# An encoder layer on one core: a second buffer for the raw weights and their sums, another order of seven products, and final norms written in place

## The chip, the cores and the metric

The kernel runs on one core of a Trainium2 chip. The metric is device time in microseconds (us) of one execution of the whole program. The engines named below are PE (TensorE, matmuls), PEld (its weight loads), DVE (VectorE), ACT (ScalarE), POOL (GpSimd) and SP (SyncE, which here only issues DMAs). Each engine works through its own queue in order; semaphores tie the queues together.

## The reference, cut to what matters

One bidirectional hybrid layer: latent attention beside a state space model, an output projection, then an MLP with a squared ReLU. The change touches only what stands from the output projection on:

```python
    h = h + rms_norm(mix @ w_out[i], g_post_mix[i])
    m = rms_norm(h, g_pre_mlp[i]) @ w_mlp_up[i]
    m = jnp.square(jax.nn.relu(m)) @ w_mlp_down[i]
    h = h + rms_norm(m, g_post_mlp[i])
return h[:, N_META:]
```

`h` has 2048 rows of 1024 columns (after the 16 meta rows are dropped), `w_mlp_up` is 1024 x 4096, `w_mlp_down` 4096 x 1024, all float32.

## The kernel before

**Precision.** Every float32 operand is split (`split`, lines 125 to 127) into a rounded part (ACT copies it, line 126) and the rest (DVE subtracts, line 127); a product is then three matmuls: high x high, high x low, low x high. In the names, `ah`/`al` and `wh`/`wl` are the two parts of a left and a right factor.

**Seven products.** Both MLP projections multiply 2 x 2 blocks with seven products instead of eight. The sums that the scheme needs are formed ahead (POOL, line 1266 for the up-projection's weights into `st`, line 1555 for the down-projection's into `wst`) and behind (DVE, POOL on the results).

**Up-projection.** The 2048 rows are two halves (`ct` 0 and 1). The activations, transposed and written to DRAM as `HTD`, are read back in four slices of 1 MB (`s_load`, tile `traw`, pool `tst` with 3 buffers), split, and summed (`b_slice`, `t_slice`, `t4_slice`) into the 28 resident pairs of tiles `TB`. Over them run 16 pairs of 128 columns of `w_mlp_up` for each half, 32 pairs in all. Most pairs are `up_pair` (line 1380 on): seven products of 12 matmuls, 84 in all, into PSUM banks pA, pB, pA, pB, pE, pF, pE. Pairs 0 and 16 are `up_pair_c` (96 matmuls in eight products, which start while slices are still being made), pair 15 is `up_pair_k` (84, ordered by slice so that slices of the next half can follow).

The factors of a pair are made by `up_prep` (line 1249 on): it loads 1 MB of weights into `raw`, forms the sums in `st` on POOL, and splits seven factors into `ah`/`al`. Pool `wraw` holds `raw` and `st` with **one** buffer each; `apool` holds nine factors. The next load of `raw` can start only when the last factor of the pair before is out of the buffer.

The results go through squared ReLU (`relu2`, lines 1352 to 1374): ACT twice, then two sums on DVE (lines 1367, 1369) and two on POOL (1371, 1373), so that the seven left factors of the down-projection are written to DRAM as `MD`, seven DMAs (line 1359) for each pair, from tiles `r` (8 buffers).

**Down-projection.** `parts` runs over 8 blocks `b` of 512 rows of `w_mlp_down` and, inside, 4 groups `g` of 512 rows of the result: 32 parts of 84 matmuls (`down`, line 1619 on; matmuls at line 1642). Each part works on two pairs of row tiles (`tp`) and makes seven products into banks A, B, A, B, E, F, E. Behind a product the results go into `acc`, which holds the whole output in SBUF: product 0 is copied by ACT (line 1648); 1 and 3 are added to that copy by DVE into `u` (lines 1650, 1659), and for `b > 0` POOL adds `u` into `acc` (line 1652 after product 1, lines 1661 and 1662 after product 3); DVE adds products 2, 4, 5, 6 (lines 1657, 1664, 1666, 1668). Line 1664 needs what line 1661 wrote. `m_factors` reads `MD` back (tile `mraw`) and splits, `w_factors` loads and makes the right factors of block `b + 1` during `g == 3`, two for each product, into a ring of `WR = 16` (14 are in use).

**Final norms.** In the last block `finish` (line 1597 on) runs once for each of the 16 row tiles: it loads the residual `HD`, squares `acc` on ACT into the second half of its buffer `fin` (line 1604), gets the scale on POOL, multiplies (DVE line 1611; ACT 1614 and POOL 1615 for the other half), adds the residual (DVE line 1616) and writes out (line 1617). There are two buffers `fin`, one for each tile in work.

A scheduler orders each engine's instructions when the program is built; the order in the code is only its starting point.

Of the kernel before, what the change touches and what calls it, by code (L numbers as in the profile page):

```python
# [51 lines left out]
def hymba_layer_kernel(  # L52
# [1119 lines left out]
    tst = hw.enter_context(pool("tst", 3))  # L1172
    wraw = hw.enter_context(pool("wraw", 1))
# [109 lines left out]
    for t in range(NT):  # L1283
        last.append((t, out_tile(t, lambda: hn_T(*last.pop(0)) if len(last) == 2 else None)))
        if t in (10, 11, 12):
            s_load(0, t - 10)
        if t >= NT - 4:
            facs.append(next(prep))
# [9 lines left out]
    upr = up_.enter_context(pool("upr", 8, "right"))  # L1298
# [14 lines left out]
    def t_slice(ct, k, eng=V):  # L1313

        raw = RAW.pop((ct, k))
        b11, b12, _, b22 = (raw[:, i] for i in range(4))
        t1, t2, t3 = rt(), rt(), rt()
        eng.tensor_tensor(out=t1, in0=b12, in1=b11, op=ALU.subtract)
        eng.tensor_tensor(out=t3, in0=b22, in1=b12, op=ALU.subtract)
        eng.tensor_tensor(out=t2, in0=b22, in1=t1, op=ALU.subtract)  # L1320
        if k == 0:
            s_load(ct, 3)
        for n, t in ((T2, t2), (T3, t3), (T1, t1)):
            split(t, *TB[n, k])
# [27 lines left out]
    def relu2(c, src, n, odd, half):  # L1352

        S.activation(out=c, in_=src, func=AF.Relu)
        S.activation(out=c, in_=c, func=AF.Square)
        md = MD[n // NP, n % NP]

        def put(i, x):
            Y.dma_start(out=md[:, i], in_=x)

        if (odd, half) != (0, 1):
            put({(0, 0): 0, (1, 0): 2, (1, 1): 5}[odd, half], c)
        blocks[odd, half] = c
        if len(blocks) == 4:
            a11, a12, a21, a22 = (blocks.pop(x) for x in ((0, 0), (1, 0), (0, 1), (1, 1)))
            s1, s2, s4 = rt(), rt(), rt()
            V.tensor_tensor(out=s1, in0=a21, in1=a22, op=ALU.add)
            put(4, s1)
            V.tensor_tensor(out=a21, in0=a11, in1=a21, op=ALU.subtract)
            put(3, a21)  # L1370
            G.tensor_tensor(out=s2, in0=s1, in1=a11, op=ALU.subtract)
            put(1, s2)
            G.tensor_tensor(out=s4, in0=a12, in1=s2, op=ALU.subtract)
            put(6, s4)
# [132 lines left out]
    for k in range(3):  # L1507
        s_load(1, k)
# [18 lines left out]
    WR = 16  # L1527
# [3 lines left out]
    def w_factors(b):  # L1531
# [9 lines left out]
        for first, *more in ((b11,), (b22, (sub, b12), (add, b11)), (b21,), (b22, (sub, b12)), (b12, (sub, b11)),  # L1541
# [55 lines left out]
    def finish(t):  # L1597
        both = wr.tile([128, 2, 1024], F32, tag="raw", name="fin")
        ht, jk = both[:, 0], both[:, 1]
        Y.dma_start(out=ht, in_=HD[t])  # L1600
        ss = sm.tile([128, 2], F32, tag="s2f", name="s2f")
        for half in range(2):
            hs = slice(half * 512, (half + 1) * 512)
            S.activation(out=jk[:, hs], in_=acc[:, t, hs], func=AF.Square, accum_out=ss[:, half:half + 1])
        st = sm.tile([128, 1], F32, tag="ss", name="ss")
        G.tensor_tensor(out=st, in0=ss[:, 0:1], in1=ss[:, 1:2], op=ALU.add)
        r = rstd_of(st, D)
        for half, eng in ((0, V), (1, G)):
            hs = slice(half * 512, (half + 1) * 512)
            if half == 0:  # L1610
                V.scalar_tensor_tensor(out=jk[:, hs], in0=acc[:, t, hs], scalar=r, in1=gpl[:, hs],
                                       op0=ALU.mult, op1=ALU.mult)
            else:
                S.activation(out=jk[:, hs], in_=acc[:, t, hs], func=AF.Copy, scale=r)
                G.tensor_tensor(out=jk[:, hs], in0=jk[:, hs], in1=gpl[:, hs], op=ALU.mult)
            V.tensor_tensor(out=jk[:, hs], in0=jk[:, hs], in1=ht[:, hs], op=ALU.add)  # L1616
            Y.dma_start(out=ov[t // 8, t % 8][:, hs], in_=jk[:, hs])

    def down(b, g, step):
# [6 lines left out]
        names = ("A", "B", "A", "B", "E", "F", "E")  # L1626
        p = [{} for _ in range(2)]
        tmp = [{n: dt_.tile([128, 512], F32, tag=n, name=n) for n in ("p1", "u2", "u3")} for _ in range(2)]
        lo, hi = slice(0, 512), slice(512, 1024)
        for i in range(7):  # L1630
            step(i, False)
            first = i in (0, 1, 4, 5)
            mh, ml = mine[i]
            for tp in range(2):
                if first:
                    p[tp][names[i]] = pa("p" + names[i])
                ps = p[tp][names[i]]
                for fp in range(2):
                    wh, wl = WF[i][fp]
                    c = 2 * fp + tp  # L1640
                    for j, (x, y) in enumerate(((mh, wh), (mh, wl), (ml, wh))):
                        T.matmul(out=ps, lhsT=x[:, c], rhs=y, start=(first and fp == 0 and j == 0),  # L1642
                                 stop=(fp == 1 and j == 2), skip_group_check=not first)
                ta, tb_ = tiles[tp]
                p1, u2, u3 = (tmp[tp][n] for n in ("p1", "u2", "u3"))
                c11, c12, c21, c22 = acc[:, ta, lo], acc[:, ta, hi], acc[:, tb_, lo], acc[:, tb_, hi]
                if i == 0:
                    S.copy(out=p1, in_=ps)
                elif i == 1:
                    V.tensor_tensor(out=u2, in0=ps, in1=p1, op=ALU.add)  # L1650
                    if b > 0:
                        G.tensor_tensor(out=c12, in0=c12, in1=u2, op=ALU.add)
                elif i == 2:
                    if b == 0:
                        S.copy(out=c11, in_=ps)
                    else:
                        V.tensor_tensor(out=c11, in0=ps, in1=c11, op=ALU.add)
                elif i == 3:
                    V.tensor_tensor(out=u3, in0=ps, in1=p1, op=ALU.add)
                    if b > 0:  # L1660
                        G.tensor_tensor(out=c22, in0=c22, in1=u3, op=ALU.add)  # L1661
                        G.tensor_tensor(out=c21, in0=c21, in1=u3, op=ALU.add)  # L1662
                elif i == 4:
                    V.tensor_tensor(out=c22, in0=ps, in1=u3 if b == 0 else c22, op=ALU.add)
                elif i == 5:
                    V.tensor_tensor(out=c21, in0=u3 if b == 0 else c21, in1=ps, op=ALU.subtract)
                else:
                    V.tensor_tensor(out=c12, in0=ps, in1=u2 if b == 0 else c12, op=ALU.add)
# [59 lines left out]
```

## Time and profile before

| | us |
|---|---|
| three executions, median | 3359.68 (3353.49 to 3363.93) |
| profiled execution, device time | 3362.8 |
| its span, first to last instruction | 3361.0 |

The span of the profiled execution leaves 1.8 us around it. The stages, by the lines that run: up to about 1855 us attention, state space model and output projection; from there to about 2636 us the up-projection; from there to the end the down-projection, whose last 105 us also hold the final norms. A view "by windows" gives, for each stretch, the length, the busy time and number of instructions of each engine, the granted TensorE clock, the DMA share and GB/s. A matmul's busy time overlaps its neighbours', so the distance from one start to the next is what it costs.

### The profile page before, as it was taken

What the parts mean: (1) busy time and instruction counts of PE and PEld (TensorE: products, weight loads), DVE (VectorE), ACT (ScalarE), POOL (GpSimd) and SP (SyncE); (2) the same over time, 40 slices, a digit from 0 to 9 for tenths busy, and PEclk for the clock granted to TensorE, in tenths of its full rate; (3) what the DMA queues carried; (4) which work ended last, traced back from release to release, by engine and by line L of the source; (5) the groups of instructions that cost most, each with busy time, mean ns of one, the idle gap of its engine ahead of it and who ended that gap; (6) DMA issues with size and microseconds to landing.
All of it is one profiled execution on the core that took longest, in us unless ns stands there. A gap on an engine that the chain in (4) does not pass through costs nothing. (4 is left out here: it accounts for less than half of the span.)

```text
span 3361.0 us, 43408 instructions
## 1 busy us (share of the span) xinstructions
PE 3039.4 (90%) x14095; PEld 2376.0 (71%) x14095; DVE 2258.6 (67%) x3259; ACT 1763.1 (52%) x3329; POOL 1813.4 (54%) x2707
## 2 busy tenths in 40 slices
PE   6999988989999999999798789888899899999995
PEld 5899855656777666787576567666677677777773
DVE  6333387667888766754465755566555678889888
ACT  4333357888777899754354443443434433333343
POOL 4122337776888876100122655557556446767776
PEclk8999989999999999999899899989999899999997
DMA  4222221210000132222465433333333433333345
GB/s 149 66 75 82 78 51 41 52 44 24 26 26 15 47 91 74 87 82 63 117 182 171 138 126 119 131 117 140 132 126 122 143 116 112 118 111 115 114 124 179
DMA packets 300452, 329.93 MB, mean 98 GB/s; under 512 B 38736, under 2 KB 240848, under 8 KB 299200
## 3 DMA queue, kind: packets, MB, share of 16 engines
q1 hardware_dynamic: 298176, 325.44, 31.9%
q8 instruction: 111, 1.82, 0.2%
q10 hardware_dynamic: 1792, 1.57, 0.2%
q14 instruction: 117, 0.96, 0.1%
q0 software_dynamic: 256, 0.14, 0.0%
HBM read 206.47 MB, written 120.52 MB: 97 GB/s over the span
## 5 line engine op out<-in xcount | busy, mean ns | idle before, releaser
L628 DVE TENSOR_TENSOR pl<-s,ph 128x512 fp32r<-128x512 f32 x512 | 350.1, 686 | 164.6 <-ACT s L627 159.3
L624 ACT ACTIVATE ph<-s 128x512 fp32r<-128x512 f32 (+1 forms) x544 | 323.4, 595 | 174.5 <-PE s L622 161.1
L575 DVE TENSOR_REDUCE mx<-mxp 128x1 f32<-128x512 f32 x512 | 342.8, 684 | 62.0 <-PE mxp L574 59.0
L1266 POOL TENSOR_TENSOR st<-raw 128x512 f32<-128x512 f32 x120 | 182.7, 1523 | 259.6 <-DMA raw<-in_w_mlp_up_dram 166.7
L627 ACT ACTIVATE s<-s 128x512 f32<-128x512 f32 x512 | 304.0, 594 | 0.7
L126 ACT CAST ah<-mraw 128x512 fp32r<-128x512 f32 x224 | 138.5, 621 | 289.9 <-DMA mraw<-MD 241.1
L127 DVE TENSOR_TENSOR al<-mraw,ah 128x512 fp32r<-128x512 f32 x224 | 235.3, 1052 | 54.9 <-ACT ah L126 50.6
L620 PE MATMUL s<-ql,kh 96*128 96x512 f32 (+1 forms) x544 | 226.3, 416 | 13.2 <-ACT ZS L938 4.9
L612 PE MATMUL X<-pl,vt 128*65 128x512 f32 x512 | 209.6, 409 | 30.2 <-DVE pl L628 28.4
L621 PE MATMUL s<-qh,kl 96*128 96x512 f32 (+1 forms) x544 | 218.0, 401 | 0.0
L622 PE MATMUL s<-qh,kh 97*128 97x512 f32 (+1 forms) x544 | 214.9, 401 | 0.7 <-DMA qh<-nm 0.7
L127 DVE TENSOR_TENSOR al<-st,ah 128x512 fp32r<-128x512 f32 x120 | 127.6, 1064 | 127.7 <-ACT ah L126 123.9
L574 PE MATMUL mxp<-kh,qh 96*128 96x512 f32 x512 | 200.3, 413 | 12.8 <-DVE mx L575 5.1
L132 POOL TENSOR_SCALAR rs_v<-ss 128x1 f32<-128x1 f32 (+1 forms) x98 | 20.5, 209 | 350.8 <-ACT kvn L325 119.0
L613 PE MATMUL X<-ph,vt 128*64 128x512 f32 x512 | 205.4, 401 | 0.0
L614 PE MATMUL X<-ph,vt 128*65 128x512 f32 x512 | 204.6, 400 | 0.0
L126 ACT CAST ah<-st 128x512 fp32r<-128x512 f32 x120 | 74.4, 620 | 208.4 <-POOL st L1266 208.2
L1555 POOL TENSOR_TENSOR wst<-raw 128x512 f32<-128x512 f32 x64 | 97.5, 1529 | 103.0 <-DVE wl L127 91.8
L127 DVE TENSOR_TENSOR al<-raw,ah 128x512 fp32r<-128x512 f32 x98 | 105.9, 1083 | 65.7 <-ACT ah L126 65.7
L620 PEld LDWEIGHTS s<-ql,kh 96*128 96x128 f32 (+1 forms) x544 | 103.5, 190 | 60.2 <-ACT ZS L938 7.1
L574 PEld LDWEIGHTS mxp<-kh,qh 96*128 96x128 f32 x512 | 100.2, 197 | 51.3 <-DVE mx L575 8.1
L648 POOL DMA_DIRECT2D rr<-RD x4 | 2.7, 663 | 246.2 <-DMA RD<-o 135.7
(970 smaller groups left out, 9950.8 us busy)
## 6 DMA issues: line engine op xcount, KB each, us to landing
MD<-r SPq DMA_DIRECT2D x224, 256.0 KB
mraw<-MD SPq DMA_DIRECT2D x224, 256.0 KB
raw<-in_w_mlp_up_dram SPq DMA_DIRECT2D x32, 1024.0 KB
xt<-in_x_dram SPq DMA_DIRECT2D x32, 512.0 KB
raw<-in_w_mlp_down_dram SPq DMA_DIRECT2D x16, 1024.0 KB
ug<-UD SPq DMA_DIRECT2D x32, 256.0 KB
HD<-o SPq DMA_DIRECT2D x16, 512.0 KB
traw<-HTD SPq DMA_DIRECT2D x8, 1024.0 KB
```

What stands on the lines that cost most here:

```text
L126: S.copy(out=h, in_=src)
L127: eng.tensor_tensor(out=l, in0=src, in1=f(h), op=ALU.subtract)
L574: T.matmul(out=p, lhsT=qs[n][0][0:96, j * 128:(j + 1) * 128], rhs=kh[0:96, b * 512:(b + 1) * 512])
L575: V.reduce_max(out=mxs[n][:, j, b:b + 1], in_=p, axis=AX.X)
L612: T.matmul(out=X[:65], lhsT=v[:, t, 0:65], rhs=pl_, start=(t == 0), stop=False)
L613: T.matmul(out=X[:64], lhsT=v[:, t, 65:129], rhs=ph_, start=False, stop=False)
L620: T.matmul(out=s[:m], lhsT=kh[0:96, cs], rhs=ql, start=True, stop=False)
L621: T.matmul(out=s[:m], lhsT=kl[:, cs], rhs=qh[0:96], start=False, stop=False)
L622: T.matmul(out=s[:m], lhsT=kh[:, cs], rhs=qh, start=False, stop=True)
L624: S.activation(out=ph_[:m], in_=s[:m], func=AF.Exp, scale=SCALE)
L627: S.activation(out=s, in_=s, func=AF.Exp, scale=SCALE)
L628: V.tensor_tensor(out=pl_, in0=s, in1=f(ph_), op=ALU.subtract)
```

## The change

1. Pool `wraw` gets two buffers (so two `raw` and two `st`), `tst` two instead of three, `upr` (tiles `r`) seven instead of eight. Slices 2 and 3 of a half are loaded when slices 0 and 1 have been used up. For the first half slice 1's sums move ahead of slice 2's splits.
2. The seven left factors in `MD` and the seven right factors get another order, and `down` uses banks X, Y, X, E, X, F, E. Bank X is read three times: after products 0, 2 and 4. Product 0 goes straight into `acc` (DVE adds for `b > 0`, ACT copies for `b == 0`), so do 1, 2 and 3; only product 4 is copied by ACT into a tile `x3`, which POOL adds twice. POOL's adds for each pair of tiles fall from three to two for `b > 0`; DVE's stay at six.
3. The ring of right factors grows to 18, and four of the 14 for the next block are made in group 2.
4. `finish` takes two row tiles for one buffer, keeps only the residual and the result there, squares into `x3` and multiplies in `acc`. In the last part the products of the first pair of tiles run before those of the second.

```diff
-    tst = hw.enter_context(pool("tst", 3))
-    wraw = hw.enter_context(pool("wraw", 1))
+    tst = hw.enter_context(pool("tst", 2))
+    wraw = hw.enter_context(pool("wraw", 2))
...
-        if t in (10, 11, 12):
+        if t in (10, 11):
             s_load(0, t - 10)
...
-    upr = up_.enter_context(pool("upr", 8, "right"))
+    upr = up_.enter_context(pool("upr", 7, "right"))
...
-        if k == 0:
-            s_load(ct, 3)
+        if k < 2:
+            s_load(ct, k + 2)
...
     t_slice(0, 0, G)
-    b_slice(0, 2)
+    t_slice(0, 1, G)
 
     def before(k):
         if k == 1:
             hn_T(*last.pop(0))
-            t_slice(0, 1, G)
+            b_slice(0, 2)
...
-    for k in range(3):
+    for k in range(2):
         s_load(1, k)
...
-    WR = 16
+    WR = 18
...
-        for first, *more in ((b11,), (b22, (sub, b12), (add, b11)), (b21,), (b22, (sub, b12)), (b12, (sub, b11)),
+        for first, *more in ((b11,), (b21,), (b22, (sub, b12), (add, b11)), (b12, (sub, b11)), (b22, (sub, b12)),
                              (b22, (sub, b12), (add, b11), (sub, b21)), (b22,)):
...
-    def finish(t):
+    def finish(ts_):
+
         both = wr.tile([128, 2, 1024], F32, tag="raw", name="fin")
-        ht, jk = both[:, 0], both[:, 1]
-        Y.dma_start(out=ht, in_=HD[t])
...
+        for i, t in enumerate(ts_):
+            Y.dma_start(out=both[:, i], in_=HD[t])
+        for i, t in enumerate(ts_):
+            ht = both[:, i]
+            ss = sm.tile([128, 2], F32, tag="s2f", name="s2f")
+            for half in range(2):
+                hs = slice(half * 512, (half + 1) * 512)
+                S.activation(out=dt_.tile([128, 512], F32, tag="x3", name="jk"), in_=acc[:, t, hs], func=AF.Square,
+                             accum_out=ss[:, half:half + 1])
...
+                c = acc[:, t, hs]
+                if half == 0:
+                    V.scalar_tensor_tensor(out=c, in0=c, scalar=r, in1=gpl[:, hs], op0=ALU.mult, op1=ALU.mult)
+                else:
+                    S.activation(out=c, in_=c, func=AF.Copy, scale=r)
+                    G.tensor_tensor(out=c, in0=c, in1=gpl[:, hs], op=ALU.mult)
+                V.tensor_tensor(out=ht[:, hs], in0=c, in1=ht[:, hs], op=ALU.add)
+                Y.dma_start(out=ov[t // 8, t % 8][:, hs], in_=ht[:, hs])
...
-        names = ("A", "B", "A", "B", "E", "F", "E")
+        banks = "XYXEXFE"
...
+            def put(c):
+                if b == 0:
+                    S.copy(out=c, in_=ps)
+                else:
+                    V.tensor_tensor(out=c, in0=ps, in1=c, op=ALU.add)
+
+            if i == 0:
+                put(c11)
+            elif i == 1:
+                V.tensor_tensor(out=c11, in0=ps, in1=c11, op=ALU.add)
+            elif i == 2:
+                put(c12)
+            elif i == 3:
+                put(c22)
+            elif i == 4:
+                p[tp]["x"] = x3 = dt_.tile([128, 512], F32, tag="x3", name="x3")
+                S.copy(out=x3, in_=ps)
+                G.tensor_tensor(out=c22, in0=c22, in1=x3, op=ALU.add)
+            elif i == 5:
+                x3 = p[tp]["x"]
+                V.tensor_tensor(out=c21, in0=x3 if b == 0 else c21, in1=ps, op=ALU.subtract)
+                if b > 0:
+                    G.tensor_tensor(out=c21, in0=c21, in1=x3, op=ALU.add)
+            else:
+                V.tensor_tensor(out=c12, in0=ps, in1=c12, op=ALU.add)
+
+        if b == NB - 1 and g == 3:
+            for tp in range(2):
+                for i in range(7):
+                    product(i, tp)
+                finish(tiles[tp])
+            return
...
-        if g == 3:
+        if g == 2:
             nwf = w_factors(b + 1) if b + 1 < NB else iter(())
...
-                if g == 3:
+                if g == 2 and i > 2:
+                    next(nwf, None)
+                elif g == 3:
                     next(nwf, None)
                     next(nwf, None)
```

**SP, first pairs of the up-projection.** A row is an instruction (x6: six alike in a row): `raw` is the weights of a pair, `traw` a slice, `MD<-r` a result. Before, from the last residual row on:

```order
L1275 DMA traw<-HTD 128x2048
L1245 DMA HTD<-raw 128x4x128 x2
L1254 DMA raw<-in_w_mlp_up_dram 128x8x256
L1275 DMA traw<-HTD 128x2048 x3
L1359 DMA MD<-r 128x512 x9
L1254 DMA raw<-in_w_mlp_up_dram 128x8x256
L1359 DMA MD<-r 128x512 x6
L1254 DMA raw<-in_w_mlp_up_dram 128x8x256
L1359 DMA MD<-r 128x512 x7
```

The change, from the same place on:

```order
L1254 DMA raw<-in_w_mlp_up_dram 128x8x256
L1275 DMA traw<-HTD 128x2048
L1245 DMA HTD<-raw 128x4x128 x2
L1254 DMA raw<-in_w_mlp_up_dram 128x8x256
L1275 DMA traw<-HTD 128x2048 x3
L1359 DMA MD<-r 128x512
L1254 DMA raw<-in_w_mlp_up_dram 128x8x256
L1359 DMA MD<-r 128x512 x8
L1254 DMA raw<-in_w_mlp_up_dram 128x8x256 x2
L1359 DMA MD<-r 128x512 x9
L1254 DMA raw<-in_w_mlp_up_dram 128x8x256
L1359 DMA MD<-r 128x512 x7
```

When nine results have been written, one of these loads has been issued before (that of pair 1), and three with the change; after 18 results it is three before, and with the change five, with the sixth next in the queue.

**DVE, one part of the down-projection with `b > 0`.** `al` is the rest of a left factor; `acc` the output; pA, pB, pE, pF, pX, pY the banks. Before:

```order
L1668 TENSOR_TENSOR acc<-pE,acc 128x512 x2
L1650 TENSOR_TENSOR u_29233<-pB,p_29232 128x512
L127 TENSOR_TENSOR al<-mraw,ah 128x512
L1650 TENSOR_TENSOR u_29236<-pB,p_29235 128x512
L127 TENSOR_TENSOR al<-mraw,ah 128x512
L1657 TENSOR_TENSOR acc<-pA,acc 128x512 x2
L127 TENSOR_TENSOR al<-mraw,ah 128x512
L1659 TENSOR_TENSOR u_29234<-pB,p_29232 128x512
L1659 TENSOR_TENSOR u_29237<-pB,p_29235 128x512
L127 TENSOR_TENSOR al<-mraw,ah 128x512
L1664 TENSOR_TENSOR acc<-pE,acc 128x512
```

The change:

```order
L1673 TENSOR_TENSOR acc<-pE,acc 128x512 x2
L127 TENSOR_TENSOR al<-mraw,ah 128x512
L1653 TENSOR_TENSOR acc<-pX,acc 128x512 x2
L127 TENSOR_TENSOR al<-mraw,ah 128x512
L1658 TENSOR_TENSOR acc<-pY,acc 128x512 x2
L127 TENSOR_TENSOR al<-mraw,ah 128x512
L1653 TENSOR_TENSOR acc<-pX,acc 128x512 x2
L1653 TENSOR_TENSOR acc<-pE,acc 128x512
L127 TENSOR_TENSOR al<-mraw,ah 128x512
L1653 TENSOR_TENSOR acc<-pE,acc 128x512
L127 TENSOR_TENSOR al<-mraw,ah 128x512
L1669 TENSOR_TENSOR acc<-acc,pF 128x512 x2
```

Bank X now leaves through DVE after products 0 and 2 (bank A left through ACT after product 0), and no row of DVE up to product 3 reads a sum that POOL made in the same part.

**SP, the end of the program.** `fin<-HD` loads a residual, `out_dram<-fin` writes half a row tile. Before:

```order
L1600 DMA fin<-HD 128x1024
L1617 DMA out_dram<-fin 128x512 x4
L1600 DMA fin<-HD 128x1024 x2
L1617 DMA out_dram<-fin 128x512 x4
L1600 DMA fin<-HD 128x1024 x2
L1617 DMA out_dram<-fin 128x512 x4
```

The change:

```order
L1601 DMA fin<-HD 128x1024 x2
L1621 DMA out_dram<-fin 128x512 x6
L1601 DMA fin<-HD 128x1024 x2
L1621 DMA out_dram<-fin 128x512 x2
L1601 DMA fin<-HD 128x1024 x2
L1621 DMA out_dram<-fin 128x512 x8
```

Before, the last two residuals are loaded behind all but the last four writes; with the change behind all but the last eight.

More of the change, by code (lines that the diff above doesn't have):

```diff
@@ L1361, in relu2 @@
         if (odd, half) != (0, 1):
-            put({(0, 0): 0, (1, 0): 2, (1, 1): 5}[odd, half], c)
+            put({(0, 0): 0, (1, 0): 1, (1, 1): 5}[odd, half], c)
         blocks[odd, half] = c
@@ L1367, in relu2 @@
             V.tensor_tensor(out=s1, in0=a21, in1=a22, op=ALU.add)
-            put(4, s1)
+            put(3, s1)
             V.tensor_tensor(out=a21, in0=a11, in1=a21, op=ALU.subtract)
-            put(3, a21)
+            put(4, a21)
             G.tensor_tensor(out=s2, in0=s1, in1=a11, op=ALU.subtract)
-            put(1, s2)
+            put(2, s2)
             G.tensor_tensor(out=s4, in0=a12, in1=s2, op=ALU.subtract)
@@ L1595, in hymba_layer_kernel @@
     Y.dma_start(out=gpl, in_=g_post_mlp[0].partition_broadcast(128))
-    def finish(t):
+    def finish(ts_):
         both = wr.tile([128, 2, 1024], F32, tag="raw", name="fin")
-        ht, jk = both[:, 0], both[:, 1]
-        Y.dma_start(out=ht, in_=HD[t])
[L1601 to L1617, printed above, removed]
@@ new lines, in finish @@
+        for i, t in enumerate(ts_):
[7 more added lines that the diff above has]
+                             accum_out=ss[:, half:half + 1])
+            st = sm.tile([128, 1], F32, tag="ss", name="ss")
+            G.tensor_tensor(out=st, in0=ss[:, 0:1], in1=ss[:, 1:2], op=ALU.add)
+            r = rstd_of(st, D)
+            for half in range(2):
+                hs = slice(half * 512, (half + 1) * 512)
+                c = acc[:, t, hs]
[6 more added lines that the diff above has]
+                Y.dma_start(out=ov[t // 8, t % 8][:, hs], in_=ht[:, hs])
@@ L1625, in down, with product @@
         del MFs[:7]
-        names = ("A", "B", "A", "B", "E", "F", "E")
+        banks = "XYXEXFE"
         p = [{} for _ in range(2)]
-        tmp = [{n: dt_.tile([128, 512], F32, tag=n, name=n) for n in ("p1", "u2", "u3")} for _ in range(2)]
         lo, hi = slice(0, 512), slice(512, 1024)
+        def product(i, tp):
+            first = i in (0, 1, 3, 5)
+            mh, ml = mine[i]
+            if first:
+                p[tp][banks[i]] = pa("p" + banks[i])
+            ps = p[tp][banks[i]]
+            for fp in range(2):
+                wh, wl = WF[i][fp]
+                c = 2 * fp + tp
+                for j, (x, y) in enumerate(((mh, wh), (mh, wl), (ml, wh))):
+                    T.matmul(out=ps, lhsT=x[:, c], rhs=y, start=(first and fp == 0 and j == 0),
+                             stop=(fp == 1 and j == 2), skip_group_check=not first)
+            ta, tb_ = tiles[tp]
+            c11, c12, c21, c22 = acc[:, ta, lo], acc[:, ta, hi], acc[:, tb_, lo], acc[:, tb_, hi]
+            def put(c):
[22 more added lines that the diff above has]
+                V.tensor_tensor(out=c12, in0=ps, in1=c12, op=ALU.add)
@@ L1630, in down @@
+        if b == NB - 1 and g == 3:
[4 more added lines that the diff above has]
+            return
         for i in range(7):
             step(i, False)
-            first = i in (0, 1, 4, 5)
-            mh, ml = mine[i]
             for tp in range(2):
[L1635 to L1668, printed above, removed]
@@ L1669, in down @@
+                product(i, tp)
             step(i, True)
         if b == NB - 1:
-            for ta, tb_ in tiles:
-                finish(ta)
-                finish(tb_)
+            for pair in tiles:
+                finish(pair)
     parts = [(b, g) for b in range(NB) for g in range(4)]
```

## The prediction

> **What bounds the kernel now.** I read the page's head first, then a view by windows over the two projections, then who makes PE wait there, and last single rows.
>
> ```profile
> span 3361.0 us, 43408 instructions
> PE 3039.4 (90%) x14095; PEld 2376.0 (71%) x14095; DVE 2258.6 (67%) x3259; ACT 1763.1 (52%) x3329; POOL 1813.4 (54%) x2707
> ```
>
> ```profile
> core 0: us, PE busy (x) PEld busy (x) DVE busy (x) ACT busy (x) POOL busy (x), PEclk, DMA share, GB/s
> 1877.00:1915.00 38.00, 24.64 (x87) 17.79 (x85) 31.79 (x30) 16.34 (x30) 29.67 (x20) 0.82 0.42 145
> 1915.00:2215.00 300.00, 269.35 (x1091) 209.22 (x1091) 168.13 (x183) 120.63 (x206) 172.85 (x118) 0.95 0.37 125
> 2215.00:2306.00 91.00, 69.80 (x266) 52.62 (x264) 71.07 (x79) 43.36 (x77) 57.36 (x36) 0.89 0.40 139
> 2306.00:2607.00 301.00, 273.88 (x1092) 213.63 (x1093) 166.77 (x183) 120.23 (x207) 175.51 (x119) 0.94 0.37 124
> 2607.00:2636.00 29.00, 26.17 (x101) 20.12 (x99) 17.62 (x20) 13.87 (x24) 13.09 (x10) 0.88 0.37 122
> 2636.00:2680.00 44.00, 30.52 (x111) 23.10 (x110) 33.12 (x41) 21.52 (x39) 22.61 (x15) 0.84 0.54 172
> 2680.00:2800.00 120.00, 117.34 (x513) 95.51 (x512) 93.31 (x129) 45.95 (x79) 53.13 (x37) 1.00 0.37 112
> 2800.00:3240.00 440.00, 418.99 (x1790) 334.44 (x1789) 388.60 (x477) 153.41 (x264) 314.08 (x205) 0.99 0.38 113
> 3240.00:3361.00 121.00, 73.74 (x282) 55.84 (x280) 100.69 (x114) 47.29 (x107) 83.56 (x88) 0.82 0.52 174
> ```
>
> PE is the busiest engine in all of these stretches, but busy time hides how far the matmuls stand apart. Single rows show that:
>
> ```profile
> 2336.62 0.50 PE L1341 MATMUL pA<-T00h,ah 128*128 128x512 f32 x1 [2.87 <-ACT ah L126]
> 2338.53 0.63 PE L1341 MATMUL pA<-T01h,ah 128*128 128x512 f32 x1
> 2338.95 0.63 PE L1341 MATMUL pA<-T01l,ah 128*128 128x512 f32 x1
> 2344.22 0.39 PE L1341 MATMUL pA<-T20h,ah 128*128 128x512 f32 x1
> 2346.94 0.39 PE L1341 MATMUL pB<-T30h,ah 128*128 128x512 f32 x1
> ```
>
> From 2344.22 to 2346.94 stand the 12 matmuls of one product: 2.72 / 12 = 0.2267 us each. That is the price of a matmul when nothing is missing. Just behind the wait of 2.87 us they stand 0.42 apart, nearly twice as far: a gap is paid again in slow matmuls behind it. By 0.2267, the 513 matmuls of the stretch from 2680 need 116.3 of its 120 us, while the 1092 from 2306 need 247.6 of 301. So the up-projection loses most. Its wait and its rhythm:
>
> ```profile
> PE pA L1341 <- ACT ah L126: 42.5, 22, 3.3
> PE pA L1341 <- DVE al L127: 11.8, 21, 0.6
> ```
>
> ```profile
> 1938.53 0.38 SPq L1254 DMA_DIRECT2D raw<-in_w_mlp_up_dram  x1
> ...
> 2215.25 0.38 SPq L1254 DMA_DIRECT2D raw<-in_w_mlp_up_dram  x1
> ...
> 2306.01 0.38 SPq L1254 DMA_DIRECT2D raw<-in_w_mlp_up_dram  x1
> ...
> 2607.06 0.38 SPq L1254 DMA_DIRECT2D raw<-in_w_mlp_up_dram  x1
> ```
>
> The first fence counts PE's waits from 1915 to 2607: some 22 pairs begin by waiting for their first factor. In the second, loads 3 and 15 lie 276.7 us apart (12 pairs, 23.06 each), loads 18 and 31 301.1 us (13 pairs, 23.16). A pair needs 84 x 0.2267 = 19.04. What ends the wait is the load:
>
> ```profile
> L1266 POOL TENSOR_TENSOR st<-raw 128x512 f32<-128x512 f32 x52 | 76.8, 1477 | 113.6 <-DMA raw<-in_w_mlp_up_dram 74.6 <-DVE al L127 39.0
> L127 DVE TENSOR_TENSOR al<-st,ah 128x512 fp32r<-128x512 f32 x52 | 55.7, 1071 | 64.4 <-ACT ah L126 62.8
> L1266 POOL TENSOR_TENSOR st<-st,raw 128x512 f32<-128x512 f32 x39 | 54.4, 1395 | 3.1
> L127 DVE TENSOR_TENSOR al<-raw,ah 128x512 fp32r<-128x512 f32 x39 | 41.0, 1052 | 29.7 <-ACT ah L126 29.7
> L1367 DVE TENSOR_TENSOR r<-r 128x512 f32<-128x512 f32 x13 | 22.6, 1741 | 0.3 <-ACT r L1355 0.3
> L1371 POOL TENSOR_TENSOR r<-r 128x512 f32<-128x512 f32 x13 | 20.3, 1559 | 8.2 <-DVE r L1367 8.2
> L1373 POOL TENSOR_TENSOR r<-r 128x512 f32<-128x512 f32 x13 | 21.8, 1674 | 0.5
> L1404 DVE TENSOR_TENSOR r<-u,pF 128x512 f32<-128x512 f32 x13 | 8.9, 686 | 6.0 <-PE pF L1341 5.9
> ```
>
> These groups cover the 13 pairs from 2306 to 2607. POOL stands 74.6 / 13 = 5.7 us a pair waiting for `raw`, and 39.0 / 13 = 3.0 for its one buffer `st`. So a pair's cycle is not PE's 19.04: it is one load plus the chain POOL, ACT, DVE over seven factors, with nothing overlapped.
>
> **Term 1, the pairs.** With two `raw`, SP's order shows the loads one to two pairs ahead, so both waits of POOL leave the cycle. Next in line are the engines themselves: POOL has (76.8 + 54.4 + 20.3 + 21.8) / 13 = 13.3 us a pair, DVE 166.8 / 13 = 12.8, ACT 120.2 / 13 = 9.2, all from the rows above. All lie under 19.04, so PE becomes the bound, with nine factor buffers as its reserve. How close it comes I take from the stretch at 2680: 116.3 / 120 = 97%, 19.04 / 0.97 = 19.6. The 601 us of the two windows hold 26 pairs: 26 x (23.1 - 19.6) = **91 us**. At best 26 x 4.06 = 105; the other end is the first rival's, 49.
>
> **Term 2, the change of halves.** The window 2215 to 2306 holds pairs 15, 16 and 17: 264 matmuls, 59.8 us, of 91. Factors made ahead take away some of the 31 us lost, but DVE was busy for 71.1 of them, with splits and sums of the slices that remain. Now slices 2 and 3 also wait for a buffer of 0 and 1, and SP stands behind that, with the writes of `MD` queued after it and only seven `r`. Not shown before: at worst one load in the open, 5.7 us as POOL sees it, at best 25 of the 31. I take **14**, near the middle.
>
> **Term 3, the first pairs.** 87 matmuls, 19.7 us, in the 38 from 1877; DVE is busy for 31.8. Loads 1 and 2 come earlier, slices 2 and 3 later (again at most a load, 5.7); DVE's work is as before. Between -6 and +10 I take **3**.
>
> **Term 4, into the down-projection.** 2607 to 2680: 212 matmuls, 48.1 us, of 73. PE waits there:
>
> ```profile
> PE pB L1642 <- ACT wh L126: 7.3, 1, 7.3
> PE pF L1642 <- ACT wh L126: 5.4, 1, 5.4
> ```
>
> The first is for the second right factor. It was a sum made by POOL and is now a plain block, so that wait should shrink; the second stays a sum that ACT splits between casts. The pair that ends in this stretch also begins with a wait of term 1's kind. **10**, between 0 and 18.
>
> **Term 5, the down-projection.** From 2800 to 3240 1790 matmuls need 405.8 of 440 us. Its waits and the POOL row that goes:
>
> ```profile
> PE pE L1642 <- DVE acc L1664: 8.8, 13, 1.7
> PE pB L1642 <- DVE u L1650: 8.2, 8, 2.0
> ```
>
> ```profile
> L1652 POOL TENSOR_TENSOR acc<-acc,u 128x512 f32<-128x512 f32 x43 | 65.0, 1524 | 56.5 <-DVE u L1650 56.5
> ```
>
> DVE is the second bound here: 388.6 of 440, 88%. It keeps six adds for each pair of tiles, at 0.69 (line 1404's row is such an add). But POOL loses one add of three: 65 us of its 314. And DVE's splits depend on what POOL does beside them:
>
> ```profile
> 2336.05 1.27 POOL L1266 TENSOR_TENSOR st<-raw 128x512 f32<-128x512 f32 x1 [6.34 <-DMA raw<-in_w_mlp_up_dram]
> ...
> 2341.99 1.77 DVE L127 TENSOR_TENSOR al<-raw,ah 128x512 fp32r<-128x512 f32 x1
> ...
> 2347.52 0.69 DVE L127 TENSOR_TENSOR al<-st,ah 128x512 fp32r<-128x512 f32 x1 [1.46 <-ACT ah L126]
> ```
>
> The same split takes DVE 0.69 or 1.77 us; a sum on POOL takes 1.27 when it runs alone and 1477 ns on the mean. With fewer adds on POOL fewer splits are long; the right factors are spread over 11 steps in place of 7, and no bank waits for POOL any more. Of the 34 us lost I take back **20** (5 to 30: the named waits alone are 17).
>
> **Term 6, the end.**
>
> ```profile
> L1604 ACT ACTIVATE fin<-acc 128x512 f32<-128x512 f32 x32 | 19.9, 623 | 44.5 <-DMA out_dram<-fin 39.6 <-DVE acc L1664 2.9 <-DVE acc L1668 1.1
> ```
>
> ACT waits 39.6 us for a buffer whose result is still being written, although it needs it only as scratch. Squaring elsewhere and four tiles in two buffers take that wait away. What is late next is DVE: 100.7 us of work in the 121, all of which stays. So 121 can fall to about 106, with some 5 us of DVE idle in the last chain: **15**, between 3 (another wait takes its place) and 25 (DVE's ops shorter as POOL works less).
>
> **Sum.** 91 + 14 + 3 + 10 + 20 + 15 = 153; all low ends 49 - 6 - 6 + 0 + 5 + 3 = 45, all high ends 213. The profiled execution took 3362.8, 3.1 over the median of 3359.7. So 3362.8 - 153 - 3 = **3207**.
>
> **Rivals.** *DVE and POOL bind the pairs* (3249). Denser pairs put POOL's ops beside more of DVE's. If each of a pair's nine DVE ops on two tiles of SBUF (seven `al`, lines 1367 and 1369) took 1.77, with four adds from a bank at 0.69, DVE would need 18.7 us; at the 88% that it reaches in the down-projection a pair takes 21.2, and term 1 is 26 x 1.9 = 49. The sum is 111. For it: line 1367 stands at 1741 ns already. Against: `al` is at 1.06 on the mean, and seven factors of reserve smooth it. The Trainium skill ("SBUF — State Buffer", section "Who interferes with whom") states a rule that speaks against the change here: DVE and GpSimd share one port pair as an exclusive lock, held for a whole instruction, so that a DVE operation with both inputs in SBUF and a GpSimd operation block each other fully. By that rule a pair whose nine DVE operations all meet a POOL operation is the one of 21.2 us, and the sum is 111; without it the sum is 153. The 1.77 beside the 0.69 agree with it.
>
> *The loads are not ahead after all* (3298). SP issues in order, and a load that waits for its buffer holds back the writes of `MD` behind it; if `r` runs out, the pair stays at 23.1. Only term 1 goes: 3362.8 - 62 - 3. Against: the load has a whole pair of slack, and seven `r` serve seven results a pair.
>
> *Bank X makes PE wait, and the kernel is slower* (3423). Product 2 needs X free of product 0, product 4 of product 2, each with one product (2.72 us) between, and both leave through DVE for `b > 0`, which is 88% busy. If two long splits (2 x 1.77) stand ahead each time, 28 parts x 2 x 3.5 = 196 us come in where term 5 gave 20: 3362.8 - 133 + 196 - 3. It turns the sign from 133 / 56 = 2.4 us a read. Against: bank B had just such a read and waited 8.2 us in 440; for: its longest wait, 2.0, is near the price.
>
> **Chances.** Forecast 0.70, bound by DVE and POOL 0.17, no loads ahead 0.06, bank X 0.04, better than all this 0.03. The range 3150 to 3275 takes in the first two with the uncertain terms of halves, start and end. A measurement tells about 0.3%, 10 us, from no change. Faster 0.93, same 0.03, slower 0.04.
>
> **What would show it.** Term 1: loads of `raw` 19 to 20 us apart, POOL without idle time for `raw`, PE clock near 1.00 from 1915. Term 5: no wait of PE for bank E, short ones for X, `al` under 1.05. Term 6: ACT without waits for `out_dram`, DVE over 90% busy to the end. I am wrong if the loads stay 21 us apart or more, or if PE's waits for X add up to over 20 us.

## The result, and the profile after

| | us | range |
|---|---|---|
| before, 4 runs | 3361.8 | 3353.5 to 3367.8 |
| after, 4 runs | 3232.4 | 3229.2 to 3232.8 |

The ratio is 0.9615, with a 95% interval from 0.9592 to 0.9637: 3.8% faster. The forecast was 3207, in a range from 3150 to 3275, so the time lies in the range, 25 us above the predicted one, which was put together from parts that missed in both directions. One execution of `ring_18_late`, below, ran at a granted clock of 0.743 and took 3671.8 us; its time there is the median of the other four.

The view by windows of the changed kernel, with the columns of before. Its up-projection ends at 2502 instead of 2636, so 2502, 2546, 2666 and 3106 answer to 2636, 2680, 2800 and 3240 of before:

```profile
core 0: us, PE busy (x) PEld busy (x) DVE busy (x) ACT busy (x) POOL busy (x), PEclk, DMA share, GB/s
...
1961.00:2145.00 184.00, 184.00 (x814) 152.38 (x813) 123.83 (x136) 88.47 (x154) 132.55 (x89) 1.00 0.47 152
...
2188.00:2244.00 56.00, 46.43 (x190) 37.00 (x189) 49.56 (x49) 25.86 (x47) 45.20 (x27) 0.91 0.44 147
2244.00:2502.00 258.00, 258.00 (x1140) 213.66 (x1139) 189.08 (x198) 128.62 (x224) 183.44 (x124) 1.00 0.48 156
2502.00:2546.00 44.00, 32.28 (x118) 24.24 (x117) 26.21 (x31) 21.46 (x39) 20.87 (x14) 0.84 0.40 124
2546.00:2666.00 120.00, 114.68 (x489) 93.20 (x489) 90.92 (x113) 48.76 (x86) 52.55 (x36) 0.97 0.39 119
2666.00:3106.00 440.00, 410.86 (x1753) 335.38 (x1752) 365.48 (x473) 151.09 (x263) 239.26 (x157) 0.97 0.37 111
3106.00:3227.00 121.00, 87.27 (x346) 67.34 (x344) 106.59 (x126) 50.33 (x115) 86.46 (x89) 0.89 0.55 185
```

PE has no gap in the pairs: 814 matmuls of 0.2267 us need 184.5 of 184 us, at a granted clock of 1.00. The up-projection, from the last write of `HD` to the down-projection's first matmul, took 782.5 us before (1853.7 to 2636.2) and takes 654.5 (1847.7 to 2502.2), 128 less. From there to the end it was 724.8 us before and is 725.2. So **128 of the 133.6 us between the two profiled executions lie in the up-projection**, and the forecast's 45 us for terms 4 to 6 did not come. The other 6 us lie ahead of it; in the experiments below that start wanders from 1845.7 to 1852.6 (one_raw apart), so they are not put down to the change. Counting matmuls by 0.2267 shows how the last 725 us come out level: the 120 us stretch does 489 instead of 513 (5.4 us worse), the 440 us stretch 1753 instead of 1790 (8.4 worse), the last 121 us 346 instead of 282 (14.5 better). Such counts are good to some 3 us.

Four groups of the page after: the copies (line 126) and splits (line 127) of left factors, the up-projection's sums (line 1266) and the first matmuls into bank X (line 1644). A row has the count, busy us, mean ns, then the idle time before them:

```profile
L126 ACT CAST ah<-mraw 128x512 fp32r<-128x512 f32 x224 | 138.8, 620 | 302.4 <-DMA mraw<-MD 216.0
L127 DVE TENSOR_TENSOR al<-mraw,ah 128x512 fp32r<-128x512 f32 x224 | 214.8, 964 | 73.5 <-ACT ah L126 68.2
L1266 POOL TENSOR_TENSOR st<-raw 128x512 f32<-128x512 f32 x120 | 179.9, 1501 | 135.2 <-DVE al L127 128.5
...
L1644 PE MATMUL pX<-wh,ah 128*128 128x512 f32 x384 | 160.2, 418 | 48.4 <-DVE acc L1653 48.1
```

POOL hardly waits for the load any more (6.7 us of the 135.2, 166.7 before), only for DVE. And PE now waits 48.1 us for bank X, which the forecast named as a sign that it is wrong (over 20 us). Six waits of 2.9 to 5.2 us, one in each block, near its start, make 26 us of it, and the last 121 us another 14. Single rows of one such place, first SP, then ACT, DVE and PE (start, length, engine, line; in brackets the idle time and what ended it):

```profile
2864.89 0.98 SPq L1537 DMA_DIRECT2D raw<-in_w_mlp_down_dram  x2
2866.65 18.32 SPq L1570 DMA_DIRECT2D mraw<-MD  x6
```

```profile
2869.77 1.14 ACT L126 CAST wh<-raw 128x512 fp32r<-128x512 f32 x2 [4.41 <-DMA raw<-in_w_mlp_down_dram]
2872.36 1.14 ACT L126 CAST wh<-raw 128x512 fp32r<-128x512 f32 x2 [1.45 <-DMA raw<-in_w_mlp_down_dram]
...
2881.52 0.62 ACT L126 CAST ah<-mraw 128x512 fp32r<-128x512 f32 x1 [6.01 <-DMA mraw<-MD]
```

```profile
2864.14 1.28 DVE L127 TENSOR_TENSOR wl<-raw,wh 128x512 fp32r<-128x512 f32 x2
...
2870.43 2.99 DVE L127 TENSOR_TENSOR wl<-raw,wh 128x512 fp32r<-128x512 f32 x2 [0.81 <-ACT wh L126]
2873.34 1.27 DVE L1669 TENSOR_TENSOR acc<-acc,pF 128x512 f32<-128x512 f32 x2
2874.54 2.38 DVE L127 TENSOR_TENSOR wl<-raw,wh 128x512 fp32r<-128x512 f32 x2
2876.84 3.48 DVE L127 TENSOR_TENSOR al<-mraw,ah 128x512 fp32r<-128x512 f32 x2
...
2882.17 1.03 DVE L127 TENSOR_TENSOR al<-mraw,ah 128x512 fp32r<-128x512 f32 x1 [0.66 <-ACT ah L126]
2883.88 0.69 DVE L127 TENSOR_TENSOR al<-mraw,ah 128x512 fp32r<-128x512 f32 x1 [0.67 <-ACT ah L126]
2884.49 1.28 DVE L1653 TENSOR_TENSOR acc<-pX,acc 128x512 f32<-128x512 f32 x2
```

```profile
2885.23 0.79 PE L1644 MATMUL pX<-wh,ah 128*128 128x512 f32 x1 [5.17 <-DVE acc L1653]
2885.82 0.63 PE L1644 MATMUL pX<-wl,ah 128*128 128x512 f32 x1
2886.25 0.63 PE L1644 MATMUL pX<-wh,al 128*128 128x512 f32 x1
```

The next block's weights (2 MB) are loaded and at once four right factors are split. DVE's queue holds four `wl` and then splits of left factors. Pairs of these take 2.4 to 3.5 us, where the pair at 2864.14 took 1.28; POOL was idle then, and works beside them from 2869.88 on. The last two splits also wait for ACT (0.66 and 0.67 us), whose copy at 2881.52 had waited 6.01 us for its load. SP could issue that load only at 2878.65, when the first of the two splits at 2876.84 had ended and freed one of the two `mraw` buffers, so a late split makes the next one late. The add that frees X stands behind all this.

### The profile page after: what moved, and what is told of

The parts are those of the page before. It is cut to its first block, busy times and chain, and to the rows that moved or that the text cites. A ratio compares the mean times of both kernels' runs of the same rounds, so it can differ in the third digit from the quotient of the medians.

```text
span 3227.4 us, 43434 instructions
## 1 busy us (share of the span) xinstructions
PE 2976.6 (92%) x14095; PEld 2361.9 (73%) x14095; DVE 2246.5 (70%) x3243; ACT 1763.7 (55%) x3345; POOL 1751.5 (54%) x2659
## 5 line engine op out<-in xcount | busy, mean ns | idle before, releaser
L127 DVE TENSOR_TENSOR al<-mraw,ah 128x512 fp32r<-128x512 f32 x224 | 214.8, 964 | 73.5 <-ACT ah L126 68.2
L1266 POOL TENSOR_TENSOR st<-raw 128x512 f32<-128x512 f32 x120 | 179.9, 1501 | 135.2 <-DVE al L127 128.5
L1666 POOL TENSOR_TENSOR acc<-acc,x 128x512 f32<-128x512 f32 x64 | 101.5, 1588 | 200.2 <-ACT x L1665 200.2
L1644 PE MATMUL pX<-wh,ah 128*128 128x512 f32 x384 | 160.2, 418 | 48.4 <-DVE acc L1653 48.1
L1644 PE MATMUL pX<-wl,ah 128*128 128x512 f32 x384 | 156.7, 408 | 0.5 <-DVE wl L127 0.4
L1644 PE MATMUL pX<-wh,al 128*128 128x512 f32 x384 | 156.2, 407 | 0.0
```

What stands on the lines that cost most here:

```text
L127: eng.tensor_tensor(out=l, in0=src, in1=f(h), op=ALU.subtract)
```

## The experiments

Each kernel was timed beside the kernel before, which had 3358.1, 3359.4 and 3360.2 in the three groups of runs; so the groups agree to about 2 us. The intervals reach some 4 to 5 us to either side, and differences below that are not shown.

| kernel | us | ratio to before, 95% |
|---|---|---|
| up_alone | 3228.2 | 0.9603 to 0.9629 |
| up_and_norms | 3223.3 | 0.9585 to 0.9611 |
| up_and_products | 3220.1 | 0.9567 to 0.9593 |
| ring_16 (up, products, norms) | 3205.8 | 0.9533 to 0.9559 |
| ring_18_late | 3229.4 | 0.9597 to 0.9628 |
| old_norms | 3240.5 | 0.9634 to 0.9660 |
| one_sum | 3242.8 | 0.9642 to 0.9669 |
| one_raw | 3330.8 | 0.9905 to 0.9932 |
| third_add | 3223.5 | 0.9579 to 0.9606 |
| x_by_scalar | 3233.6 | 0.9613 to 0.9639 |
| four_mraw | 3195.1 | 0.9499 to 0.9525 |
| low_halves_gpsimd | 3179.8 | 0.9449 to 0.9478 |

### Which buffer: one_sum and one_raw

```diff
-st = wraw.tile([128, 4, 128], F32, tag="st", name="st")
+st = wraw.tile([128, 4, 128], F32, tag="st", name="st", bufs=1)        # one_sum
-raw = wraw.tile([128, 8, 256], F32, tag="raw", name="raw")
+raw = wraw.tile([128, 8, 256], F32, tag="raw", name="raw", bufs=1)     # one_raw; and so the tile `hn` of the last row tile
```

> The changed kernel, with one buffer for the left factors' sums instead of two (two raw buffers stay). Theory A, the second raw buffer carries the up-projection's gain: the pairs stay at 19.0 to 20.0 us and the time lies between 3232 and 3262 us. Theory B, the second sum buffer carries it, since GpSimd may then go ahead of VectorE's split: the pairs go back to 22 to 23 us and the time to 3320 to 3350 us. If both are needed, the time lies between.

> The changed kernel, with one buffer for the raw left weights instead of two (two sum buffers stay). Theory A, the second raw buffer carries the gain, because the load of a pair's weights no longer starts only behind the last read of the pair before: the pairs go back to 22.5 to 23.1 us, the time to 3232 + 26 x 3.5 = 3323 us or some 18 us more where the change of halves loses its gain too (3341 us). Theory B, the second sum buffer carries it: 19.0 to 20.0 us a pair, 3232 to 3262 us.

POOL's waits from 1961 to 2188 us (total, times, longest), first with one sum buffer, then with one raw buffer:

```profile
POOL st L1266 <- DVE al L127: 41.7, 34, 1.9
...
POOL st L1266 <- DMA raw<-in_w_mlp_up_dram: 6.0, 1, 6.0
```

```profile
POOL st L1266 <- DMA raw<-in_w_mlp_up_dram: 68.1, 11, 6.6
POOL st L1266 <- DVE al L127: 19.7, 16, 1.8
```

With one `raw` the wait is back, 6.2 us a pair (68.1 / 11), and the kernel takes 3330.8, 98 us more than the changed one. Not all of that is the pairs': in the profiled execution the up-projection takes 742.3 us (1868.5 to 2610.9), 88 more, so 88 of the 128 us are lost again. It also starts 21 us later. Its instructions stand in another order from the attention part on, and why that part got longer was not looked into. With one `st` 10 us are lost. Theory A holds; the second sum buffer adds a little.

### The parts apart: up_alone, up_and_norms, up_and_products, old_norms

up_alone is the kernel before with the up-projection's lines of the change, among them these; up_and_norms adds the new `finish` and the last part's loop over `tp`, up_and_products the new order and banks instead. old_norms is the changed kernel without its norms.

```diff
-    tst = hw.enter_context(pool("tst", 3))
-    wraw = hw.enter_context(pool("wraw", 1))
+    tst = hw.enter_context(pool("tst", 2))
+    wraw = hw.enter_context(pool("wraw", 2))
...
-        if k == 0:
-            s_load(ct, 3)
+        if k < 2:
+            s_load(ct, k + 2)
```

> The kernel before with the up-projection's part of the change alone (raw and sum buffers, tiles of the right operand, order of its slices and of the products written out); the down-projection and the final norms are the old ones, and so is the ring of right factors. Theory C, the down-projection's part and the norms together give nothing (the new products lose about 14 us in the middle, the new end gains about 14): 3232 us, within 6. Theory D, by the forecast's terms 4 to 6 the rest is worth 45 us: 3277 us. In the trace theory C wants 790 to 800 matmuls in each 184 us of the steady down-projection or more, as before, and the last 121 us with some 282 matmuls as before instead of 346.

> The kernel before with the up-projection's part of the change and the new final norms (two tiles a buffer, in place, the last part one pair of tiles after the other), but with the old order and old banks of the down-projection's products. Theory C, the new products lose 14 us in the middle and the new end gains 14.5 by itself: 3232 - 14 = 3218 us. Theory E, the end gains only because the new products leave VectorE and GpSimd freer there, so norms and products go together: 3232 us. If the new products gain (forecast's term 5, 20 us): 3252 us.

> The changed kernel with the old final norms (one tile a buffer, beside a second tile) and with the last part's two pairs of tiles side by side in each product, as before the change. By the count of matmuls in the last 121 us the new end is worth 14.5 us: 3247 us, from 3240 to 3255. If the end is set by VectorE's work whatever the order, 3232 us.

> The kernel before with the up-projection's part and the new order of products alone: ring of 16 right factors, made in the last part of a block, and the old final norms with the last part's pairs of tiles side by side. If the products' gain (3223 - 3206 = 17 us at the new norms) stands by itself and the norms are worth 5 to 8 us: 3211 to 3214 us. If products and norms only gain together: 3223 us or more.

up_alone takes 3228.2: what the change does behind the up-projection is worth nothing, or costs 4 us, which is within the noise; theory C holds. (The 790 to 800 matmuls in 184 us that the expectation names are no figure of the kernel before, which has 1790 in 440 us; up_alone has 1798.) The norms alone were worth 4.9 us with the old products (3228.2 to 3223.3), between the two theories, and 8.1 in the changed kernel (old_norms), less than counted in the window. up_and_products, too, lies between its two cases, 8.1 below up_alone. With products and norms, ring_16 takes 3205.8: 22.4 less than up_alone, where 8.1 and 4.9 would give 13.0. That they do more together than apart is likely but not shown: by the ratios it is 23.5 us against 18.1, and each of the four ratios has an interval of 4 to 5 us to either side.

### What the ring costs: ring_16 and ring_18_late

```diff
-    WR = 18
+    WR = 16                                  # ring_16 alone
-        if g == 2:
+        if g == 3:                           # both
             nwf = w_factors(b + 1) if b + 1 < NB else iter(())
...
-                if g == 2 and i > 2:
-                    next(nwf, None)
-                elif g == 3:
+                if g == 3:
```

> The changed kernel with a ring of 16 right factors instead of 18, and the next block's factors made in the last part of a block alone, as before the change. It is the control for the next two runs, for which it frees 8 KB a partition. Theory F, the wider ring did not spread the factors' work (all 14 still stand in two of four parts): within 6 us of 3232, and TensorE's waits for bank X stay at about 70 us. Theory G, the four early factors crowd VectorE where X is read: 3215 to 3226 us and X's waits under 40 us.

> The changed kernel with the ring of 18, but with the next block's factors asked for only in the last part of a block, as before the change. Theory W, the width of the ring alone makes the loss, since the scheduler places a factor as soon as the ring has room: 3226 to 3236 us, as the changed kernel. Theory V, the four early requests make it: 3203 to 3215 us.

The wide ring loses 26.6 us (3232.4 to 3205.8), or 23.6 by ring_18_late; ring_16 is faster than even theory G had it. The requests in the code lose nothing: in ring_18_late's trace DVE, ACT and SP run the same instructions in the same order as in the changed kernel's, so the scheduler places a factor as the ring has room, whenever it is asked for. (The 70 us that some expectations give X's waits is not PE's figure, which is 48.1.) PE's waits for X fall from 48.1 to this in ring_16:

```profile
PE pX L1644 <- DVE acc L1653: 26.2, 17, 4.1
```

The loads of two blocks' weights, four blocks apart, of the changed kernel and of ring_16 give the time of a block:

```profile
2696.97 0.97 SPq L1537 DMA_DIRECT2D raw<-in_w_mlp_down_dram  x2
...
3035.57 0.98 SPq L1537 DMA_DIRECT2D raw<-in_w_mlp_down_dram  x2
```

```profile
2702.40 2.53 SPq L1537 DMA_DIRECT2D raw<-in_w_mlp_down_dram  x2
...
3023.99 0.46 SPq L1537 DMA_DIRECT2D raw<-in_w_mlp_down_dram  x1
```

338.6 / 4 = 84.7 us against 321.6 / 4 = 80.4; a block's 336 matmuls need 76.2. The 4.3 us a block are less than what one big wait for X costs with its slow matmuls (7.3 us, last section). So the wide ring did not spread the factors: it moved two more of a block's 14 up to the very start of the block before, into the rows shown above, where four are split at once; in ring_16 two are. At the place shown, the load that ACT waited for took 2.9 us from issue (2878.65) to copy (2881.52), no longer than the next but one (2883.24 to 2886.12), so the crowd in DVE's queue is the nearer cause there and not the 2 MB of weights. Over the kernel the two were not separated.

### What X waits for: x_by_scalar and four_mraw

Both start from ring_16, which frees their space.

```diff
+                elif i == 3:
+                    V.tensor_tensor(out=c, in0=ps, in1=c, op=ALU.add)
                 else:
-                    V.tensor_tensor(out=c, in0=ps, in1=c, op=ALU.add)
+                    xa = dt_.tile([128, 512], F32, tag="xa", name="xa")
+                    S.copy(out=xa, in_=ps)
+                    V.tensor_tensor(out=c, in0=xa, in1=c, op=ALU.add)
```

```diff
-    mst = ctx.enter_context(pool("mst", 2))
+    mst = ctx.enter_context(pool("mst", 4))
```

> The control, and the first and third product's sums are read out of bank X by ScalarE into a tile (tag xa, two buffers), from which VectorE adds them to acc; only from the second block on, and all sums are still computed. Theory T, TensorE waits since X comes free only after an add that stands behind other work in VectorE's queue: the waits of pX for acc all but vanish (under 10 us of 70) and the time falls by 20 to 50 us against the control. Rival R1, the queues are late because of the two mraw buffers (ScalarE waits for a load, VectorE for ScalarE): ScalarE's copy then stands behind the same wait, and the time stays within 8 us of the control. Rival R2, VectorE's throughput is the bound: no gain, or a loss of up to 20 us, since VectorE keeps its adds.

> The control with four mraw buffers instead of two. Rival R1, the left factors' loads make ScalarE late and by it VectorE: ScalarE's waits for mraw (about 200 us in all) fall under 80 us, the waits of pX for acc under 30 us, and the time falls by 15 to 40 us against the control. Theory T alone (the order in VectorE's queue, whatever the loads): X's waits stay above 50 us, the time within 8 us of the control.

Theory T fell: x_by_scalar is 27.8 us **slower** than ring_16, of the sign that R2 had and beyond its 20 us. PE's waits for X moved to ACT, and the add got dearer, first in x_by_scalar, then in ring_16:

```profile
L1644 PE MATMUL pX<-wh,ah 128*128 128x512 f32 x384 | 154.5, 406 | 24.0 <-ACT xa L1656 22.3 <-DVE acc L1662 1.7
...
L1657 DVE TENSOR_TENSOR acc<-xa,acc 128x512 f32<-128x512 f32 x112 | 113.5, 1014 | 0.0
```

```profile
L1653 DVE TENSOR_TENSOR acc<-pX,acc 128x512 f32<-128x512 f32 x112 | 73.2, 678 | 5.4 <-PE pX L1644 5.4
```

From SBUF the same add takes 1014 ns instead of 678, 40.3 us more in all (113.5 - 73.2). Other groups of DVE got shorter, so that its busy time over the whole kernel rises by 22.0 us (2246.8 to 2268.8 by the pages). Four `mraw` gain 10.8 us, between the numbers of the two theories. Its groups of left factors and of X:

```profile
L126 ACT CAST ah<-mraw 128x512 fp32r<-128x512 f32 x224 | 137.8, 620 | 183.2 <-PE pX L1644 89.0 <-PE pE L1644 39.2 <-PE pY L1644 28.1
...
L1644 PE MATMUL pX<-wh,ah 128*128 128x512 f32 x384 | 153.6, 402 | 18.2 <-DVE acc L1653 18.2
```

ACT's waits for the loads, 196.7 us in ring_16, are no longer among the three largest, so 28 us at most. Yet PE still waits 18.2 us for X, of 26.2: the loads carry a part, and something else the rest.

### Whose time is it: third_add and low_halves_gpsimd

third_add puts one more GpSimd add a pair of tiles into ring_16; low_halves_gpsimd moves three of seven subtractions for right factors from VectorE to GpSimd in four_mraw.

```diff
+                    xd = dt_.tile([128, 512], F32, tag="xd", name="xd")
+                    G.tensor_tensor(out=xd, in0=x3, in1=gpl[:, lo], op=ALU.add)   # third_add
...
-                split(src, h, l)
+                split(src, h, l, V if more else G)                              # low_halves_gpsimd
```

> The run with a ring of 16, and behind each sixth product from the second block on one more GpSimd add of 128 x 512, of x3 and the norm's weights into a tile that nothing reads (56 in all, some 85 us of GpSimd's time): GpSimd has three adds for a pair of tiles again, as before the change. Theory P, the new products gain since GpSimd is freer: 3215 to 3224 us, and TensorE's waits grow. Theory Q, they gain by the order in which banks are read and by fewer waits of VectorE, and GpSimd was never the bound: 3203 to 3210 us.

> The run with four mraw buffers, and the low halves (wl) of the three right factors that are raw blocks are made by GpSimd instead of VectorE (6 of 14 a block, each about 0.7 us of VectorE and about 1.5 us of GpSimd). Theory R2, what is left (about 25 us of TensorE in the steady part) is VectorE's throughput: 3183 to 3192 us. Rival, GpSimd's adds beside VectorE's lengthen VectorE's subtractions and right factors come late: 3195 to 3215 us, with more waits for wl or wst.

third_add takes 17.7 us more than ring_16, as theory P had it. Groups of the page's kind, two of ring_16 and then three of third_add:

```profile
L127 DVE TENSOR_TENSOR al<-mraw,ah 128x512 fp32r<-128x512 f32 x224 | 220.7, 990 | 64.7 <-ACT ah L126 63.9
...
L1653 DVE TENSOR_TENSOR acc<-pX,acc 128x512 f32<-128x512 f32 x112 | 73.2, 678 | 5.4 <-PE pX L1644 5.4
```

```profile
L127 DVE TENSOR_TENSOR al<-mraw,ah 128x512 fp32r<-128x512 f32 x224 | 241.5, 1083 | 57.1 <-ACT ah L126 55.6
...
L1673 POOL TENSOR_TENSOR xd<-x,gpl 128x512 f32<-128x512 f32 x56 | 85.3, 1523 | 0.0
L1653 DVE TENSOR_TENSOR acc<-pX,acc 128x512 f32<-128x512 f32 x112 | 73.1, 677 | 2.6 <-PE pX L1644 2.6
```

85.3 us of POOL, for which nobody waits, make DVE's split of two SBUF tiles 93 ns longer, 224 times, or 20.8 us; the add that reads a bank stays at 677 ns. The Trainium skill ("SBUF — State Buffer", section "Who interferes with whom") states just that: a VectorE instruction with two inputs in SBUF contends with a GpSimd instruction that reads SBUF, one with at most one such input does not. The rows agree.

The other way round, low_halves_gpsimd takes 48 subtractions from DVE, which in four_mraw were this group:

```profile
L127 DVE TENSOR_TENSOR wl<-raw,wh 128x512 fp32r<-128x512 f32 x48 | 54.4, 1141 | 9.6 <-ACT wh L126 9.6
```

It gains 15.3 us on four_mraw: 3179.8, the shortest time of all kernels here and below the 3183 to 3192 of theory R2. The steady stretch, by windows, in ring_16, four_mraw and low_halves_gpsimd:

```profile
2666.00:3106.00 440.00, 420.81 (x1818) 342.71 (x1817) 379.05 (x488) 157.33 (x272) 249.03 (x166) 0.99 0.39 115
```

```profile
2666.00:3106.00 440.00, 421.53 (x1831) 344.85 (x1830) 380.17 (x490) 157.96 (x277) 258.53 (x168) 0.99 0.40 119
```

```profile
2666.00:3106.00 440.00, 429.63 (x1885) 352.88 (x1885) 359.76 (x475) 166.47 (x298) 314.58 (x215) 1.00 0.40 125
```

1885 matmuls need 427.3 of 440 us, DVE falls to 359.8, and POOL can take 314.6 without being the bound. PE's waits for X fall from 18.2 us to 7.2. So DVE's time weighs on the down-projection: three runs that change its busy time over the whole kernel (third_add by +21.3 us, x_by_scalar by +22.0, low_halves_gpsimd by -45.4) move the result the same way (+17.7, +27.8, -15.3). That it is the only limit is not shown. The three are not in proportion, x_by_scalar also puts the release of X into ACT's queue, and four_mraw gains its 10.8 us with DVE as busy as in ring_16 (2248.2 and 2246.8 us).

## Why the prediction was right or wrong

- **Term 1, the pairs: right, sized low.** Before, the 601 us lost 106.1 us over 0.2267 a matmul; after, nothing: 106 instead of 91. The step that erred is the 97% borrowed from the down-projection. The loads lie 19.2 us apart (ten pairs from 1952.83 on). The cause is shown by one_raw, where 88 us of the up-projection's 128 are lost again. The rival with DVE and POOL as bounds fell: DVE is busy for 123.8 of 184 us. That 3232 lies nearer to its 3249 than to 3207 is chance.
- **Term 2, the change of halves: right.** 56 us for 190 matmuls lose 12.9 instead of 31.2: 18, against 14.
- **Term 3: right.** What is left of the 128 us is about -2, against 3 and within its -6 to +10: 128 less 106, 18 and the 6 us that the stretch from 2607 to 2636 had lost (29 less 101 x 0.2267).
- **Term 4: right.** Those 6 and seven matmuls more in the first 44 us (1.6): 8, against 10.
- **Term 5, the down-projection: wrong in sign.** Counted by matmuls -14 instead of +20. Two of its three reasons held: POOL's lost add does shorten DVE's splits, and no bank waits for POOL. With the old ring the products are worth 8.1 us beside the old norms and 17.5 beside the new (up_and_norms to ring_16). The step that failed is "the right factors are spread over 11 steps in place of 7". It was read from the code; the scheduler fills the wider ring as soon as it can, which costs 24 to 27 us.
- **Rival bank X: the mechanism was there, the price was not.** PE waits 48.1 us for X, but in 20 waits, up to 5.2 us, not 56 times 3.5. That is 0.9 a read, under the 2.4 at which the sign would turn. And it was not the third read of X as such: at a ring of 16 the same banks wait 26.2 us and the kernel gains.
- **Term 6, the end: right by the window, half by the run.** 14.5 us counted, 8.1 by old_norms, 14.3 with a ring of 16 (up_and_products to ring_16), against 15. ACT waits no longer for `out_dram`; DVE is busy for 88% to the end, not over 90.
- **Two readings that do not hold.** PE is not the busiest engine in all nine stretches: DVE is in those from 1877, 2215, 2636 and 3240 (100.7 us against 73.7 in the last). And POOL's sum of 1.27 us at 2336.05 does not run alone: a split of DVE starts at 2336.59 and takes 1.28. Neither enters the sum.

Terms 1 and 2 came out 19 us above the forecast, term 5 some 34 below, terms 3 and 4 together 7 below: by the terms' own counts 131 us, 22 short of the 153. That the time came out within 25 us is in part luck, since the misses of terms 1 and 5 have opposite signs. The profiled executions differ by 133.6 us, 19 short. Of the 25 us the other 6 are the choice of execution: the forecast took 3 us off for the profiled one before, and the profiled one after lies 3.3 us below its median.

## What to carry to other kernels

A second buffer is worth a whole load's wait when the loop that it feeds has one chain from load to last reader; count the loop's other engines and expect the bound to go all the way to the next one. Where a scheduler orders the queues, a wider ring is no plan for spreading work: look at the order that it produces, since early work lands in a bunch and in-order queues put it ahead of what frees a bank. And the cost of an engine off the critical path may lie in its neighbour: count the operations of VectorE with two SBUF inputs that stand beside GpSimd's.

## What the runs showed of the hardware

How dear a wait of PE is depends on its length. Behind a wait of 1.50 us the matmuls go on at 0.23, behind 5.17 they stand 0.43 apart (rows at 2885.82 and 2886.25) until 2889.59. The rows of the changed kernel:

```profile
2867.28 0.50 PE L1644 MATMUL pX<-wh,ah 128*128 128x512 f32 x1 [1.50 <-DVE acc L1653]
2867.61 0.40 PE L1644 MATMUL pX<-wl,ah 128*128 128x512 f32 x1
2867.84 0.40 PE L1644 MATMUL pX<-wh,al 128*128 128x512 f32 x1
...
2889.59 0.40 PE L1644 MATMUL pX<-wl,ah 128*128 128x512 f32 x1
2889.82 0.40 PE L1644 MATMUL pX<-wh,al 128*128 128x512 f32 x1
```

The ten matmuls from 2885.23 to 2889.59 took 4.36 us instead of 2.27, so the long wait cost 7.3 us, not 5.2. In the rows of both projections of eight traces (before, the changed kernel, up_alone, ring_16, third_add, x_by_scalar, four_mraw, low_halves_gpsimd), taking only waits behind 20 matmuls without a gap and with no gap among the next 16, none of 21 waits from 1.25 to 2.03 us was followed by more than 0.2 us of delay, and 24 of 26 from 2.53 to 5.33 us were followed by 1.5 to 3.0 us (waits from start to start, less 0.2267). How the two others stayed cheap is open.
